# Moving half of a value projection, twelve top-key rounds, four zero fills and six weight splits between stages and engines of a hybrid decoder layer

## The chip, the cores and the metric

The kernel runs on one core of one Trainium2 chip. The time is the device time of one execution in microseconds (us), and a kernel's time is the median of its runs. The trace comes from one profiled execution. The engines are TensorE (PE, with its weight loads PEld), VectorE (DVE), ScalarE (ACT), GpSimd (POOL) and SyncE (SP, which issues most of the DMAs). Each engine works through its own instructions in the order in which the program lists them.

## The reference, cut to what matters

One decoder layer on 512 tokens of 1024 features, in float32. One input projection feeds two mixers side by side, an mLSTM (4 heads) and a sparse attention (8 heads, the 128 keys of highest indexer score per query). Their outputs go through one output projection, then a gated MLP with a width-3 convolution and a final norm.

```python
z = rms_norm(x) @ w_in                    # 1024 -> 3664 columns, split into:
# m_q, m_k (256 each), m_v, m_o (512 each), gates, a_q, a_k, a_v (512 each), indexer q, k, w
qk = silu(causal_dwconv(concat(m_q, m_k)))            # width 4
hm = mlstm_chunkwise(q, k, m_v, m_i + i_bias, m_f + f_bias)
hm = sigmoid(m_o) * rms_norm(hm)
score = sum_h relu(q_idx[h] @ k_idx.T / 8) * w_idx[h]  # causal
idx = top_k(score, 128)                                # then attention over these keys only
ha = softmax(a_q @ a_k[idx].T / 8 + rel_bias) @ a_v[idx]
x = x + concat(hm, ha) @ w_out
```

The top keys are not gathered: for each block of 128 queries the kernel strikes out the eight largest scores sixteen times and keeps as a mask which keys were struck.

## The kernel before, in words

Tokens go in four blocks of 128 (t = 0 to 3). A float32 product is made of three products of split operands: `split` rounds a tile to the high part on ScalarE (L122) and subtracts it for the low part (L123), on VectorE, or on GpSimd for weights whose index is in `on_pool`. Weight columns come in by DMA (`raw`, 1 MB each) and are split in pieces ahead of use: `take` hands out the split pieces of a step and puts the splits of later ones into a queue `later`, of which one entry is run after each step.

The order of the work is written out by `merge`: a list of main steps spread evenly over 0 to 1, and side lists with a range of their own; all are sorted by their place. `fm_steps` (four steps for 128 output columns, each 6 matmuls of 512 columns) and `tm_steps` (eight steps for 256 output columns, each 12 matmuls of 256 columns) make the main steps. The stages around the change are:

- the indexer's query stage (`to_iq`), with the first steps of `idx_steps` (the indexer's scores) beside it;
- the stage of the attention's projections (`to_aq`, `to_ak`, `to_av`), with the rest of the indexer's steps, the gates' first part, and the top keys of t = 1, 2 and the first part of t = 3 (`top_steps`: 16 times max, L510, and strike, L513, and then `keep`, L516). `att_[0]`, the ready step, makes the first queries and the first `ql` pair (`second`, L657);
- the attention's stage: four convolution projections (`to_conv`, 16 steps) and the mLSTM values (`to_mv`, 8 steps for each half), with the rest of the top keys of t = 3 and the attention's steps beside them. An attention step i puts the scores of item i (t, head) into one of three `lg` banks (L670 to L673), makes the numerators of item i - 1 (L695 on VectorE, L698 on ScalarE), transposes those of item i - 3 and multiplies those of item i - 4 with the values (L711). `second` makes the low part of the queries, two L657 for two heads. For t = 3, L704 on GpSimd needs the last `keep`. After the convolutions `silus` runs SiLU on `mq` and `mk`;
- the output gates' stage (`to_mo`, 16 steps), with the mLSTM's decays (`decays[2:]`), the split queries and keys (`parts`: L825 and L826 for keys, L834 to L836 for queries, L816 for the zeros that fill the other half of the low queries), the score steps (`qks`: two matmuls L844, L845, evicted at L847, L850), and the transposition of the attention's output (`to_mix`);
- the output projection and the mLSTM's heads, and then the MLP, which the change doesn't touch.

The stages are not separated by barriers: each engine goes on as far as its operands are there. The split indices are: 17 to 20 convolution, 21 to 24 values, 25 to 28 output gates, 29 to 36 output projection.

Of the kernel before, what the change touches and what calls it, by code (L numbers as in the profile page):

```python
# [11 lines left out]
F32R = mybir.dt.float32r  # L12
BF = mybir.dt.bfloat16
AF = mybir.ActivationFunctionType
OP = mybir.AluOpType

S, D, DFF, NB = 512, 1024, 2816, 4
# [27 lines left out]
def hybrid_layer(ctx: ExitStack, tc: tile.TileContext, a, out):  # L45
# [44 lines left out]
    def merged(main, *sides):  # L90
        merge(main, *sides, later=later)
        while later:
            later.popleft()()
# [84 lines left out]
    for c2 in range(NF // 2):  # L178
        add_raw(rows(a["w_down"], 2 * c2), [row_cut(0), row_cut(1)])
    sub_i, look = [0], [2]  # L180
    on_pool = set(range(6, 31)) | {35,37,39}

    def take(n=1):

# [317 lines left out]
    def top_steps(t):  # L502
        w = (t + 1) * 128
        acc = score[t][:, :w]

        m8 = {}

        def largest():
            m8[0] = small.tile([128, 8], F32, name="m8")
            nc.vector.max(m8[0], acc)  # L510

        def strike():
            nc.vector.match_replace(acc, m8[0], acc, TAKEN)  # L513

        def fin():
            nc.vector.tensor_scalar(keep[t][:, :w], acc, TAKEN, -BIG, op0=OP.not_equal, op1=OP.mult)  # L516
        return [largest, strike] * 16 + [fin]
# [86 lines left out]
    for c in range(4):  # L604
        main += fm_steps(H, to_iq(c), tok=((128, 512),))
    idx = idx_steps()
    merged(main, (0.0, 0.02, [params_consts]), (0.5, 0.55, [params_bias]), (0.0, 0.02, [misc_a]), (0.18, 0.2, [misc_b]),
          (0.3, 1.05, idx[:18]), (0.8, 0.85, [params_conv]))

    kS = big.tile([128, 8, S], F32R, name="kS", tag="B0")  # L610

# [21 lines left out]
    def zeros():  # L633
        nc.gpsimd.tensor_scalar(qlz.rearrange("p a b c -> p (a b) c"), ident[:, None, :].to_broadcast([128, 4, 128]), 0.0,
                                None, op0=OP.mult)

    def att_steps(ts):
# [14 lines left out]
        def second(p):  # L652

            t, c = divmod(p, 4)
            src = aqT[:, c, t * 128:(t + 1) * 128]
            for i, a_ in ((0, slice(0, 64)), (1, slice(64, 128))):
                nc.vector.tensor_tensor(qlz[a_, p % 2, i, :], src[a_], qp[p // 2][a_, c % 2, i, :].bitcast(F32), OP.subtract)  # L657

        def step(i):
            if i % 4 == 1 and i // 4 + 1 < n // 4:  # L660
                queries(i // 4 + 1)
            if i % 2 == 0 and i // 2 + 1 < n // 2:
                second(i // 2 + 1)
            if i < n:
                t, h = items[i]
# [56 lines left out]
        def costed(i):  # L722
            def f():
                step(i)
            f.cost = items[min(i, n - 1)][0] + 2.947
            return f
        def ready():
            zeros()
            queries(0)
            second(0)  # L730
        return [ready] + [costed(i) for i in range(n + 4)]

    main = []
# [2 lines left out]
    for c in range(4):  # L736
# [2 lines left out]
    att_ = att_steps(range(NB))  # L739
    top3 = top_steps(3)  # L740
    mm_tags[:] = ["mm", "mm", "av"][:3]
    merged(main, (0.0, 0.07, idx[18:]), (0.3, 0.5, gates_a), (0.07, 0.32, top_steps(1)), (0.32, 0.68, top_steps(2)),
           (0.68, 1.0, top3[:18]), (0.3, 0.32, [params_bias2]), (0.75, 0.76, [att_[0]]))


    mv = ap.tile([128, NB, 4, 130], F32, name="mv")
# [12 lines left out]
    def to_mv(c2):  # L759
        return lambda t, pz: nc.scalar.activation(mv[:, t, 2 * c2:2 * c2 + 2, :128],  # L760
                                                  pz.rearrange("p (h d) -> p h d", h=2), AF.Copy)
# [19 lines left out]
    def weight_steps():  # L781
# [28 lines left out]
        def zeros(h):  # L810

            b_ = own[h % 2][1]
            if h == 0:
                ql["two"] = ap.tile([128, 2, S], F32R, name="mql", tag="mk")
            ql[h] = ql["two"][:, h, :] if h < 2 else ap.tile([128, S], F32R, name="mql", tag=("ql", "score3")[h - 2])
            nc.gpsimd.tensor_scalar(ql[h][b_].rearrange("p (t c) -> p t c", t=NB),  # L816
                                    ident[b_, None, :].to_broadcast([64, NB, 128]), 0.0, None, op0=OP.mult)

        def keys(h):
            if h == 0:  # L820
                zeros(2)
                zeros(3)
            a_, b_ = own[h % 2]
            kh[h], src = part(h), mk[a_, h // 2, :]
            nc.scalar.activation(kh[h][a_], src, AF.Copy)  # L825
            nc.vector.tensor_tensor(kh[h][b_], src, kh[h][a_].bitcast(F32), OP.subtract)  # L826
            if h == 3:
                zeros(0)
                zeros(1)

        def queries(h):
            a_, b_ = own[h % 2]
# [24 lines left out]
    main = []  # L857
    for c in range(4):
        main += fm_steps(H, to_conv(c))
    for c2 in range(2):  # L860
        main += tm_steps(H, to_mv(c2))
    merged(main, (0.0, 0.32, top3[18:]), (0.403, 0.74, gates_b), (0.781, 0.957, decays[:2]), (0.7, 0.7, [silus]), (0.007, 1.0, att_[1:]))


    def head_steps(pair):
# [39 lines left out]
    def to_mix(src, mix, t):  # L905
        pt = bank("tp")
        for j in range(4):
            nc.tensor.transpose(pt[:, j * 128:(j + 1) * 128], src[:, j, :], ident)
        sl = slice(t * 128, (t + 1) * 128)
        split(mix[:, 0, :, sl], mix[:, 1, :, sl], pt.rearrange("p (j c) -> p j c", j=4))  # L910

    mm_tags[:] = ["mm", "mm", "av"]
    main = []
    for c2 in range(2):
        main += tm_steps(H, to_mo(c2))
    merged(main, (0.0, 0.057, decays[2:]), (0.1, 0.586, parts), (0.482, 1.0, qks),
           (0.238, 0.839, [lambda t=t: to_mix(ha[t], mixa, t) for t in range(NB)]))

    def gate_out(t):
        nc.scalar.activation(so[:, t, :], so[:, t, :], AF.Sigmoid)  # L920
# [201 lines left out]
```

## Time and profile before

| | |
|---|---|
| median of 3 runs (lowest to highest) | 688.69 us (688.48 to 689.21) |
| the profiled execution | 688.66 us, its span 686.9 us |
| mean granted TensorE clock | 0.986 of full speed |
| busy: TensorE, VectorE, ScalarE, GpSimd | 657.9, 404.6, 297.5, 169.1 us |

Times in the views are microseconds from the start of the span. A busy TensorE may still run at a lower clock, so its busy time is read together with the granted clock: 1.00 is 2.4 GHz and 0.50 is 1.2 GHz. VectorE's busy time includes the time in which a started instruction stands still.

### The profile page before, as it was taken

Reading aid. Unit: us, or ns where it says so; the run is one execution under the profiler, and the core shown is the slowest. Engines: PE = TensorE matmul, PEld = TensorE weight load, DVE = VectorE, ACT = ScalarE, POOL = GpSimd, SP = SyncE. Lnnn points to the kernel's source line nnn. Section 1 sums busy time; section 2 is a strip of 40 time slices with the busy share of each in tenths; the row PEclk is TensorE's granted clock in tenths of the full one; section 3 lists DMA queues with packets and bytes.
Section 4 is the critical chain, followed back from the end, with each engine's and each line's share of the span. In section 5 each row is a group of like instructions: output and inputs, shape, how many; then the busy total and the mean of one; then the engine's idle time right before and its main releaser. Section 6 shows DMA issues by size and latency. Waiting matters only on the chain.

```text
span 686.9 us, 8960 instructions
## 1 busy us (share of the span) xinstructions
PE 657.9 (96%) x3455; PEld 561.8 (82%) x3455; DVE 404.6 (59%) x735; ACT 297.5 (43%) x512; POOL 169.1 (25%) x166
## 2 busy tenths in 40 slices
PE   7999999699999779999999999999999999999996
PEld 5987889478999779889988888888888888888885
DVE  4689999896645766567456655555555653222234
ACT  5556265266573705345344444444444442111123
POOL 2132576132451814324010110101011020000023
PEclk9999999899999979999999999999999999999999
DMA  9321633011101111051132233311333133313102
GB/s 304 111 64 61 210 98 123 0 63 62 62 1 62 62 62 62 1 154 62 61 105 80 64 120 122 124 61 62 123 123 121 62 139 138 123 63 121 61 31 92
DMA packets 47194, 62.22 MB, mean 91 GB/s; under 512 B 3795, under 2 KB 40855, under 8 KB 47152
## 3 DMA queue, kind: packets, MB, share of 16 engines
q1 hardware_dynamic: 45488, 56.83, 24.9%
q0 software_dynamic: 944, 3.25, 1.5%
q10 hardware_dynamic: 720, 1.57, 0.6%
q8 instruction: 27, 0.44, 0.3%
q14 instruction: 15, 0.12, 0.1%
HBM read 59.53 MB, written 2.12 MB: 90 GB/s over the span
## 4 chain that ended last, share of the span: by engine, by line
PE 80%; DVE 14%; issue 2%; ACT 2%; POOL 1%; DMA 1%; POOLq 0%; DVEq 0%; ACTq 0%
PE bank_mm L192 9%; PE bank_mm L194 9%; PE bank_mm L193 9%; PE bank_av L194 4%; PE bank_av L192 4%; PE bank_av L193 4%; DVE score L513 4%; DVE m L510 3%; PE bank_av L711 2%; PE bank_lg L1051 2%; PE bank_lg L1052 2%; PE bank_lg L1050 2%; DVE score L495 2%; PE bank_mm L236 2%; PE bank_mm L237 2%; PE bank_mm L238 2%
## 5 line engine op out<-in xcount | busy, mean ns | idle before, releaser
L123 DVE TENSOR_TENSOR wlo<-raw,whi 128x1024 fp32r<-128x1024 f32 x72 | 89.4, 1246 | 118.5 <-ACT whi L122 118.5
L122 ACT ACTIVATE whi<-raw 128x1024 fp32r<-128x1024 f32 x100 | 104.6, 1051 | 85.4 <-PE bank_mm L1051 73.4
L192 PE MATMUL bank_mm<-fh,whi 128*128 128x512 f32 (+1 forms) x256 | 96.3, 376 | 0.0
L194 PE MATMUL bank_mm<-fh,wlo 128*128 128x512 f32 (+1 forms) x256 | 96.2, 376 | 0.0
L193 PE MATMUL bank_mm<-fl,whi 128*128 128x512 f32 (+1 forms) x256 | 96.2, 376 | 0.0
L123 POOL TENSOR_TENSOR wlo<-raw,whi 128x1024 fp32r<-128x1024 f32 x28 | 68.8, 2468 | 80.4 <-ACT whi L122 59.0
L1015 POOL TENSOR_TENSOR yc<-yc 128x512 f32<-128x512 f32 x22 | 28.4, 1292 | 213.4 <-DVE yc L999 213.4
L193 PEld LDWEIGHTS bank_mm<-fl,whi 128*128 128x128 f32 x256 | 48.2, 188 | 8.8
L194 PEld LDWEIGHTS bank_mm<-fh,wlo 128*128 128x128 f32 x256 | 48.2, 188 | 8.8
L192 PEld LDWEIGHTS bank_mm<-fh,whi 128*128 128x128 f32 x256 | 48.2, 188 | 8.6
L192 PE MATMUL bank_av<-fh,whi 128*128 128x512 f32 (+1 forms) x120 | 45.1, 376 | 0.0
L194 PE MATMUL bank_av<-fh,wlo 128*128 128x512 f32 (+1 forms) x120 | 45.0, 375 | 0.0
L193 PE MATMUL bank_av<-fl,whi 128*128 128x512 f32 (+1 forms) x120 | 45.0, 375 | 0.0
L192 PE MATMUL bank_mm<-hh,whi 128*128 128x512 f32 (+1 forms) x112 | 44.0, 393 | 0.0
L122 ACT ACTIVATE gh<-yc 128x512 fp32r<-128x512 f32 x22 | 13.9, 632 | 69.5 <-POOL yc L1015 69.5
L123 DVE TENSOR_TENSOR gl<-yc,gh 128x512 fp32r<-128x512 f32 x22 | 15.2, 693 | 47.4 <-ACT gh L122 47.4
L194 PE MATMUL bank_mm<-hh,wlo 128*128 128x512 f32 (+1 forms) x112 | 42.5, 380 | 0.0
L193 PE MATMUL bank_mm<-hl,whi 128*128 128x512 f32 (+1 forms) x112 | 42.4, 379 | 0.0
L236 PE MATMUL bank_mm<-whi,hh 128*128 128x256 f32 x128 | 38.8, 303 | 0.0
L237 PE MATMUL bank_mm<-whi,hl 128*128 128x256 f32 x128 | 37.2, 291 | 0.0
L238 PE MATMUL bank_mm<-wlo,hh 128*128 128x256 f32 x128 | 37.2, 291 | 0.0
L1008 ACT ACTIVATE yc<-yc 128x512 f32<-128x512 f32 x22 | 13.9, 632 | 42.6 <-DVE yc L999 42.6
(324 smaller groups left out, 1541.3 us busy)
## 6 DMA issues: line engine op xcount, KB each, us to landing
raw<-in_w_up_dram SPq DMA_DIRECT2D x22, 1024.0 KB, 5.1
raw<-in_w_in_dram SPq DMA_DIRECT2D x13, 1024.0 KB, 5.0
raw<-in_w_down_dram SPq DMA_DIRECT2D x11, 1024.0 KB, 5.0
raw<-in_w_out_dram SPq DMA_DIRECT2D x4, 1024.0 KB
T<-skew POOLq DMA_DIRECT2D x1, 2048.0 KB, 8.6
x<-in_x_dram SPq DMA_DIRECT2D x3, 512.0 KB, 5.4
out_dram<-xn SPq DMA_DIRECT2D x4, 256.0 KB, 2.1
out_dram<-xn ACTq DMA_DIRECT2D x4, 256.0 KB, 2.5
```

Of the source, the lines that this page charges most:

```text
L122: nc.scalar.activation(hv, src, AF.Copy)
L123: (eng or nc.vector).tensor_tensor(lv, src, hv.bitcast(F32), OP.subtract)
L192: nc.tensor.matmul(ps_, lh, rh, start=first, stop=False)
L193: nc.tensor.matmul(ps_, lh, rl, start=False, stop=False)
L194: nc.tensor.matmul(ps_, ll, rh, start=False, stop=last)
L236: nc.tensor.matmul(st["ps"], ah, wh[:, i, :], start=(k == 0), stop=False)
L237: nc.tensor.matmul(st["ps"], al, wh[:, i, :], start=False, stop=False)
L238: nc.tensor.matmul(st["ps"], ah, wl[:, i, :], start=False, stop=(k == 7))
L510: nc.vector.max(m8[0], acc)
L513: nc.vector.match_replace(acc, m8[0], acc, TAKEN)
L1008: nc.scalar.activation(ys[c][:, 0, :], ys[c][:, 0, :], AF.Silu)
L1015: nc.gpsimd.tensor_tensor(y[:, 0, :], y[:, 0, :], y[:, 1, :], OP.mult)
```

## The change

Half of the mLSTM values (`to_mv(1)`, eight main steps) are projected at the start of the output gates' stage and no longer in the attention's stage. Of the 33 top-key steps of t = 3, six and not eighteen come ahead of the attention's stage, and the other 27 are spread over its first half; before, the last 15 were spread over its first 0.32. The two index steps 16 and 17 go from the indexer's stage to the next. The second `ql` pair is made in the ready step and not in the attention's first step. The zeros of the low queries are made by ScalarE (a copy with scale 0) and not by GpSimd, and heads 0 and 1 now use the tiles that are free early, heads 2 and 3 the tile of the keys. The splits 25 to 30 go from GpSimd to VectorE.

```diff
@@ -178,7 +178,7 @@
     for c2 in range(NF // 2):
         add_raw(rows(a["w_down"], 2 * c2), [row_cut(0), row_cut(1)])
     sub_i, look = [0], [2]
-    on_pool = set(range(6, 31)) | {35,37,39}
+    on_pool = set(range(6, 25)) | {35,37,39}
 
     def take(n=1):
 
@@ -605,7 +605,7 @@
         main += fm_steps(H, to_iq(c), tok=((128, 512),))
     idx = idx_steps()
     merged(main, (0.0, 0.02, [params_consts]), (0.5, 0.55, [params_bias]), (0.0, 0.02, [misc_a]), (0.18, 0.2, [misc_b]),
-          (0.3, 1.05, idx[:18]), (0.8, 0.85, [params_conv]))
+          (0.3, 1.0, idx[:16]), (0.8, 0.85, [params_conv]))
 
     kS = big.tile([128, 8, S], F32R, name="kS", tag="B0")
 
@@ -659,7 +659,7 @@
         def step(i):
             if i % 4 == 1 and i // 4 + 1 < n // 4:
                 queries(i // 4 + 1)
-            if i % 2 == 0 and i // 2 + 1 < n // 2:
+            if i and i % 2 == 0 and i // 2 + 1 < n // 2:
                 second(i // 2 + 1)
             if i < n:
                 t, h = items[i]
@@ -728,6 +728,7 @@
             zeros()
             queries(0)
             second(0)
+            second(1)
         return [ready] + [costed(i) for i in range(n + 4)]
 
     main = []
@@ -739,8 +740,8 @@
     att_ = att_steps(range(NB))
     top3 = top_steps(3)
     mm_tags[:] = ["mm", "mm", "av"][:3]
-    merged(main, (0.0, 0.07, idx[18:]), (0.3, 0.5, gates_a), (0.07, 0.32, top_steps(1)), (0.32, 0.68, top_steps(2)),
-           (0.68, 1.0, top3[:18]), (0.3, 0.32, [params_bias2]), (0.75, 0.76, [att_[0]]))
+    merged(main, (0.0, 0.1, idx[16:]), (0.3, 0.5, gates_a), (0.1, 0.34, top_steps(1)), (0.34, 0.7, top_steps(2)),
+           (0.7, 0.97, top3[:6]), (0.3, 0.32, [params_bias2]), (0.75, 0.76, [att_[0]]))
 
 
     mv = ap.tile([128, NB, 4, 130], F32, name="mv")
@@ -810,23 +811,23 @@
         def zeros(h):
 
             b_ = own[h % 2][1]
-            if h == 0:
+            if h == 2:
                 ql["two"] = ap.tile([128, 2, S], F32R, name="mql", tag="mk")
-            ql[h] = ql["two"][:, h, :] if h < 2 else ap.tile([128, S], F32R, name="mql", tag=("ql", "score3")[h - 2])
-            nc.gpsimd.tensor_scalar(ql[h][b_].rearrange("p (t c) -> p t c", t=NB),
-                                    ident[b_, None, :].to_broadcast([64, NB, 128]), 0.0, None, op0=OP.mult)
+            ql[h] = ql["two"][:, h - 2, :] if h >= 2 else ap.tile([128, S], F32R, name="mql", tag=("ql", "score3")[h])
+            nc.scalar.activation(ql[h][b_].rearrange("p (t c) -> p t c", t=NB),
+                                 ident[b_, None, :].to_broadcast([64, NB, 128]), AF.Copy, scale=0.0)
 
         def keys(h):
             if h == 0:
-                zeros(2)
-                zeros(3)
+                zeros(0)
+                zeros(1)
             a_, b_ = own[h % 2]
             kh[h], src = part(h), mk[a_, h // 2, :]
             nc.scalar.activation(kh[h][a_], src, AF.Copy)
             nc.vector.tensor_tensor(kh[h][b_], src, kh[h][a_].bitcast(F32), OP.subtract)
             if h == 3:
-                zeros(0)
-                zeros(1)
+                zeros(2)
+                zeros(3)
 
         def queries(h):
             a_, b_ = own[h % 2]
@@ -857,9 +858,8 @@
     main = []
     for c in range(4):
         main += fm_steps(H, to_conv(c))
-    for c2 in range(2):
-        main += tm_steps(H, to_mv(c2))
-    merged(main, (0.0, 0.32, top3[18:]), (0.403, 0.74, gates_b), (0.781, 0.957, decays[:2]), (0.7, 0.7, [silus]), (0.007, 1.0, att_[1:]))
+    main += tm_steps(H, to_mv(0))
+    merged(main, (0.0, 0.5, top3[6:]), (0.403, 0.74, gates_b), (0.781, 0.957, decays[:2]), (0.7, 0.7, [silus]), (0.007, 1.0, att_[1:]))
 
 
     def head_steps(pair):
@@ -910,11 +910,11 @@
         split(mix[:, 0, :, sl], mix[:, 1, :, sl], pt.rearrange("p (j c) -> p j c", j=4))
 
     mm_tags[:] = ["mm", "mm", "av"]
-    main = []
+    main = tm_steps(H, to_mv(1))
     for c2 in range(2):
         main += tm_steps(H, to_mo(c2))
-    merged(main, (0.0, 0.057, decays[2:]), (0.1, 0.586, parts), (0.482, 1.0, qks),
-           (0.238, 0.839, [lambda t=t: to_mix(ha[t], mixa, t) for t in range(NB)]))
+    merged(main, (0.0, 0.05, decays[2:]), (0.08, 0.5, parts), (0.42, 1.0, qks),
+           (0.16, 0.6, [lambda t=t: to_mix(ha[t], mixa, t) for t in range(NB)]))
 
     def gate_out(t):
         nc.scalar.activation(so[:, t, :], so[:, t, :], AF.Sigmoid)
```

## Rows read from the trace of the kernel before

**Rows 1.** The page's busy times: us, share of the span, instructions.

```profile
PE 657.9 (96%) x3455; PEld 561.8 (82%) x3455; DVE 404.6 (59%) x735; ACT 297.5 (43%) x512; POOL 169.1 (25%) x166
```

**Rows 2.** Windows: stretch, length; busy of PE, PEld, DVE, ACT, POOL; clock; DMA.

```profile
116.80:128.00 11.20, 4.67 (x23) 3.38 (x22) 10.68 (x24) 3.33 (x5) 3.19 (x3) 0.87 0.10 35
128.00:132.00 4.00, 3.79 (x12) 3.12 (x12) 3.79 (x16) 1.67 (x7) 0.79 (x2) 0.51 0.00 0
132.00:137.00 5.00, 5.00 (x35) 4.32 (x34) 2.26 (x8) 3.09 (x10) 0.00 (x0) 1.00 0.00 0
137.00:155.30 18.30, 17.12 (x102) 14.01 (x101) 17.88 (x47) 10.97 (x34) 6.97 (x8) 1.00 0.18 59
233.00:248.00 15.00, 7.74 (x34) 6.98 (x35) 13.08 (x16) 4.76 (x7) 9.66 (x6) 0.66 0.36 135
218.90:262.00 43.10, 35.64 (x247) 33.06 (x246) 31.45 (x62) 18.02 (x25) 17.67 (x10) 0.88 0.14 50
```

**Rows 3.** Waits of TensorE: line, releaser, us in total, times, longest.

```profile
PE bank_lg L671 <- DVE ql L657: 6.1, 1, 6.1
PE bank_tp L844 <- DVE sc L850: 4.0, 1, 4.0
...
PE bank_tp L844 <- ACT part L835: 1.8, 1, 1.8
```

**Rows 4.** Timeline of GpSimd and VectorE, 104 to 156 us: start, length, instruction.

```profile
108.74 4.82 POOL L123 TENSOR_TENSOR wlo<-raw,whi 128x1024 fp32r<-128x1024 f32 x2
...
110.30 3.42 DVE L657 TENSOR_TENSOR ql<-qv,qd 64x128 fp32r<-64x128 f32 x2
...
126.41 0.59 DVE L657 TENSOR_TENSOR ql<-qv,qd 64x128 fp32r<-64x128 f32 x2
...
154.60 0.67 DVE L516 TENSOR_SCALAR keep<-score 128x512 bf16<-128x512 f32 x1
```

**Rows 5.** Timeline of ScalarE, VectorE and GpSimd in the output gates' stage.

```profile
226.95 2.57 ACT L825 ACTIVATE part<-mk 64x512 fp32r<-64x512 f32 x4
...
227.59 4.34 DVE L826 TENSOR_TENSOR part<-mk,part 64x512 fp32r<-64x512 f32 x2 [3.42 <-ACT part L825]
...
231.47 6.79 POOL L816 TENSOR_SCALAR mql<-ident 64x512 fp32r<-64x512 f32 x4
...
237.34 6.09 DVE L836 TENSOR_TENSOR mql<-mq,part 64x512 fp32r<-64x512 f32 x1
...
238.24 4.65 POOL L123 TENSOR_TENSOR wlo<-raw,whi 128x1024 fp32r<-128x1024 f32 x2
...
244.66 0.69 DVE L836 TENSOR_TENSOR mql<-mq,part 64x512 fp32r<-64x512 f32 x1
```

**Rows 6.** VectorE's groups by shape, 107 to 175 us: busy, mean ns, idle before.

```profile
L510 DVE MAX8 m<-score 128x8 f32<-128x512 f32 x16 | 11.1, 693 | 0.4
L513 DVE MATCH_REPLACE8 score<-m,score 128x512 f32<-128x512 f32 x16 | 10.8, 676 | 0.0
L695 DVE CUSTOM_DVE_ANT_0 l<-bank_lg,T 128x384 f32<-128x384 f32 x7 | 3.8, 555 | 0.1
```

**Rows 7.** Timeline of TensorE, six places of the attention's stage.

```profile
153.81 0.48 PE L192 MATMUL bank_mm<-hh,whi 128*128 128x512 f32 x1
...
155.28 0.34 PE L670 MATMUL bank_lg<-kS,qd 128*128 128x384 f32 x1
...
156.40 0.48 PE L192 MATMUL bank_mm<-hh,whi 128*128 128x512 f32 x1
...
175.57 0.34 PE L670 MATMUL bank_lg<-kS,qd 128*128 128x384 f32 x1
...
177.02 0.36 PE L236 MATMUL bank_mm<-whi,hh 128*128 128x256 f32 x1
...
178.53 0.39 PE L670 MATMUL bank_lg<-kS,qd 128*128 128x512 f32 x1
```

**Rows 8.** The page's group of weight splits on VectorE.

```profile
L123 DVE TENSOR_TENSOR wlo<-raw,whi 128x1024 fp32r<-128x1024 f32 x72 | 89.4, 1246 | 118.5 <-ACT whi L122 118.5
```

## The prediction, made before the result was known

> **What bounds the kernel now.** The busy table of the page comes first: TensorE is busy 96% of the span [rows 1]. So only three things can give time: the places where TensorE stands still, where it runs at the lower clock, and where another engine holds it up. The list of waits, TensorE's alone, names the places [rows 3]: 6.1 us on VectorE's `ql` (L657), and waits of the score step L844, 4.0 us on VectorE and 1.8 us on ScalarE. The windows place them [rows 2]. The first lies where the attention starts: from 116.8 to 128.0 us TensorE is busy 4.67 us of 11.20, then has 3.79 us of work at a mean clock of 0.51, that is at the lower level (1.2 GHz), which costs half of it, 1.9; a further 1.2 us are missing up to 155.3. Together 6.5 + 1.9 + 1.2 = 9.6 us. The others lie in the output gates' stage: from 233 to 248 us 7.3 us are missing, and a mean clock of 0.66 means that about 10.2 us of the window ran at the lower level; 4.0 of these were the last wait, so some 6.2 us of work cost 3.1 extra. Together 10.4 us. The prize is therefore about 20 us, in two places with different causes.
>
> **Why TensorE waits at the start of the attention.** VectorE is busy 10.68 of 11.20 us there and 17.88 of 18.30 in the window after [rows 2]. The second `ql` pair stands in VectorE's order behind rounds of max and strike, and starts only at 126.41 [rows 4], 6 us after TensorE came to it. VectorE stays the late engine until the last top-key instruction, the `keep` of L516, at 154.6 [rows 4].
>
> **Why it waits in the gates' stage.** VectorE's subtractions there are slow: two of L826 take 4.34 us, one of L836 takes 6.09, where the one at 244.66, of the same size, takes 0.69. Both long ones lie under GpSimd's work: two splits of 4.65 us begin at 238.24 and end at 242.89, and the 6.09 us end at 243.43 [rows 5]. The same is seen earlier: the `ql` pair at 110.30 takes 3.42 us in place of 0.59 and ends just behind GpSimd's split pair (108.74 to 113.56) [rows 4]. A subtraction from SBUF on VectorE stands still while GpSimd is inside an instruction. The Trainium skill's page "SBUF — State Buffer" (section "SBUF: two separate sides") has the rule: the shared port pair is an exclusive lock, and a VectorE instruction with two SBUF inputs waits for a GpSimd one that reads SBUF. By that rule a zero made by GpSimd costs VectorE up to its full length and one by ScalarE costs it nothing; the trace agrees with the first half, and the sum below uses the rows alone.
>
> **The change, gates' stage.** Four zeros of 6.79/4 = 1.7 us leave GpSimd [rows 5] and come to ScalarE; the nearest row is L825, 64x512 by ScalarE, 2.57/4 = 0.64 each, so 2.6 us. Six splits (indices 25 to 30) go from GpSimd (2.3 us each [rows 5]) to VectorE (1.24 each [rows 8]): 7.5 us, all in this stage. The second half of the values adds eight steps of TensorE. Such a step takes 178.53 - 177.02 = 1.51 us with the change of kind [rows 7], about 1.45 among its like: 11.6 us, which leave the attention's stage, so their sum is zero. What they bring is cover: the first score step stood after 8 of 16 main steps and now stands after 11 of 24, 4.4 us later, and the queries that it needs come at nearly the same place. The zeros for heads 0 and 1 now go where no keys have to be read first.
> VectorE's load over the stage: 31.45 us of 43.10 before [rows 2], less about 8.7 of standing still (4.34 - 1.37 = 3.0, 6.09 - 0.69 = 5.4, 0.3 elsewhere), plus 7.5: 30. ScalarE: 18.0 [rows 2], plus zeros 2.6, two more splits 2.1 (they fell in the stage before) and four evictions 1.5: 24. TensorE has 43.1 - 10.4 + 11.6 = 44. So nothing is near TensorE, and GpSimd does almost nothing there. I give back 1 us for a score step that finds a 1.24 us split ahead of its eviction on VectorE. Gain: 10.4 - 1 = 9.4 us; bounds 10.4 (all of it) and 5 (only the last wait goes, with half of the clock's cost, and the earlier waits come back as ScalarE's longer queue).
>
> **The change, attention's stage.** Twelve of the top-key instructions for the last rows, 0.69 (max) and 0.68 (strike) each [rows 6], go from ahead of the attention into its first half: 8.2 us. Nothing is saved on VectorE; what matters is what else is in its queue ahead of `keep`. I write out both orders by the fractions of `merged`. Before, `keep` stands between attention steps 14 and 15; after, between 20 and 21. The attention has three `lg` banks, so TensorE can't start step j before VectorE has done step j - 2. Before, `keep` ends at 155.3 and TensorE just then starts step 16 (the 384-wide L670 at 155.28 [rows 7]); after, at that moment it can start step 22. In between lie
> - TensorE: six attention steps from 1.12 us (155.28 to 156.40) to 1.45 (175.57 to 177.02) [rows 7], 7.9 in all; two more convolution steps of 1.47 (153.81 to 155.28) [rows 7], 2.9; a gate step 0.2. Sum 11.0 us.
> - VectorE: six evictions of at most 0.56 [rows 6] with their accumulator reads, 3.3 less the two narrower ones' 0.2, 3.1; three `ql` pairs of 0.59 [rows 4], 1.8; one output scaling 0.9 and the gate step 0.9 (estimates from their place in the same timeline). Sum 6.7 us.
> So `keep` would end at 155.3 + 6.7 = 162.0 with the same idle as before. VectorE stood idle 5.00 - 2.26 = 2.7 us from 132 to 137 [rows 2], because TensorE came back at 1.2 GHz; with strikes at hand and no such stop, I take half of that back: 160.6. The `ql` pairs of step 0 and 2 are now both in the first part, where GpSimd's split pair blocked one before by 2.8 us; it may block two or none, so that is zero with a bound of 2.8 either way. Gain: 11.0 - (160.6 - 155.3) = 5.7, less 0.7 for the tighter hand-over at the end, where the SiLUs now follow the last convolution by two steps: 5.0 us. Bounds: 9.6 (TensorE never waits) and 0 (`keep` comes 5.7 later through blocked pairs and waits of VectorE on TensorE).
> The remaining edits (two index steps later, the second `ql` pair in the ready step) I cost at nothing: VectorE's queue up to the first max holds the same instructions, and TensorE, which reaches the attention 2 us or more ahead of VectorE, covers them; without that cover it is two evictions, 1.1 us.
>
> **Sum.** The profiled execution took 688.66 us (span 686.9 and 1.8 around it), the median is 688.69: the same. 688.7 - 9.4 - 5.0 = 674.3 us.
>
> **Rivals.**
> *VectorE takes the whole gain of the attention's stage.* The wait is not removed, it is spread: top-key rounds stand denser among the evictions. For it: VectorE at 17.88 of 18.30 us [rows 2] with fewer rounds per step than it will have. Against: the sums 11.0 and 6.7. Time: 688.7 - 9.4 = 679.3.
> *All stops go in both stages.* For it: the work sums, if blocking by GpSimd in the first half ends too. Against: VectorE's total before `keep`. Time: 688.7 - 9.6 - 10.4 = 668.7.
> *ScalarE becomes late in the gates' stage.* Keys, queries and zeros all pass through it; 1.8 us were already a wait on it [rows 3]. Half of that stage's gain stays away: 688.7 - 5 - 5 = 678.7.
> *Slower: the clock falls in the first half of the attention.* If TensorE follows VectorE in short stops, it may be granted 1.2 GHz through them. From 116.8 to 160.6 it has about 38 us of work in 44; each us of work at the lower level costs 1 us more, so with 6 us of slack and 14.4 gained, the change loses from 20 us of work at 1.2 GHz on; with 26 us of it the time is 674.3 + 20 = 694.3. Against it: from 137 to 155.3 TensorE stood still 1.2 us in pieces and the clock stayed 1.00; it fell to 0.51 only behind the 6.1 us stop [rows 2, 3]. The Trainium skill, "TensorE: Matmul & The Clock Gate", section "A second HAM failure mode: psum-queue depth-cycling", tells of just this: frequent small stops between groups made the clock swing between its levels. No row here shows it for small stops.
>
> **Numbers.** The forecast 0.50; VectorE takes the gain 0.19; all stops go 0.11; ScalarE late 0.12; clock 0.08. The first four are all faster; 0.02 of them is kept for no change, when both lower bounds meet. A run of this kernel can tell about 0.2% (1.4 us). Faster 0.90, same 0.02, slower 0.08. Range 668.5 to 682.5: the forecast with its bounds and the three faster rivals, with 0.08 for the clock and the rest for tails outside.
>
> **What would show it.** Right: no GpSimd zero, and no split by it in the gates' stage; L826 and L836 at about 0.7 us each; no TensorE wait above 1 us at L844/L845; clock 1.00 through that stage. At the start of the attention, no 6 us wait on L657, but several of under 1.5 us on VectorE, and `keep` near 160 to 161. Wrong: `keep` later than 164, a clock of 0.5 anywhere between 117 and 260 us, or ScalarE as the releaser of L844.

## The result and the profile after

The changed kernel takes 680.59 us (median of 4 runs, 680.08 to 681.01), the kernel before in the same session 688.85 (688.48 to 689.21): a ratio of 0.988, 95% interval 0.9863 to 0.9897. It is 8.3 us faster; 14.4 were forecast. The profiled execution took 681.01 us, with a span of 679.3.

The page's busy row of the changed kernel, to be held against [rows 1]:

```profile
PE 656.2 (97%) x3455; PEld 560.0 (82%) x3455; DVE 398.9 (59%) x741; ACT 299.8 (44%) x516; POOL 147.5 (22%) x156
```

TensorE's waits in the changed kernel, 100 to 262 us (answers to [rows 3]):

```profile
PE bank_tp L845 <- DVE mixa L123: 4.8, 1, 4.8
PE bank_av L711 <- ACT pT L686: 2.7, 4, 0.7
PE bank_lg L670 <- DVE nm L695: 1.0, 2, 0.6
PE bank_tp L681 <- ACT l L698: 0.8, 1, 0.8
PE bank_av L711 <- DVE qv L718: 0.4, 1, 0.4
```

The 6.1 us stop at the start of the attention is gone; what is left there are stops of at most 0.8 us. In the gates' stage three waits became one, at the second score step, of 4.8 us. Lines behind the diff have moved by one: L826 is now L827, L836 is L837, L844 is L845.

Windows of the changed kernel (columns as in [rows 2]): the first half of the attention up to the `keep`, the rest of that stage, the gates' stage, and 2 us pieces around its stop.

```profile
116.80:159.50 42.70, 39.01 (x238) 32.07 (x237) 39.38 (x118) 26.16 (x76) 11.88 (x15) 1.00 0.11 36
159.50:203.96 44.46, 43.27 (x320) 38.57 (x319) 24.94 (x63) 28.67 (x56) 18.51 (x16) 1.00 0.15 48
203.96:254.07 50.11, 45.27 (x340) 43.95 (x339) 30.32 (x68) 22.88 (x34) 1.27 (x2) 0.93 0.18 64
...
222.00:224.00 2.00, 0.86 (x6) 0.42 (x4) 0.99 (x3) 1.96 (x3) 0.00 (x0) 1.00 0.00 0
224.00:226.00 2.00, 0.00 (x0) 0.00 (x0) 2.00 (x3) 1.95 (x4) 0.00 (x0) 1.00 0.00 0
226.00:228.00 2.00, 0.30 (x1) 0.30 (x2) 2.00 (x5) 1.72 (x3) 0.00 (x0) 0.64 0.30 31
228.00:230.00 2.00, 2.00 (x9) 2.00 (x9) 1.61 (x4) 0.00 (x0) 0.00 (x0) 0.50 0.87 354
230.00:232.00 2.00, 2.00 (x11) 2.00 (x11) 0.69 (x3) 0.00 (x0) 0.00 (x0) 0.50 0.34 139
```

The clock is 1.00 through the whole attention's stage. Behind the stop of the gates' stage it is at the lower level (0.50, 1.2 GHz) from 228 to 232 us. While TensorE stands still, from 222 to 226 us, ScalarE is busy in both pieces, 1.96 and 1.95 of 2.00 us; VectorE is in the second, 2.00, but only 0.99 in the first.

The timeline of the changed kernel, at places that answer to [rows 4, 5, 7], and then the stop itself:

```profile
107.94 3.46 DVE L657 TENSOR_TENSOR ql<-qv,qd 64x128 fp32r<-64x128 f32 x4
...
159.11 0.43 DVE L516 TENSOR_SCALAR keep<-score 128x512 bf16<-128x512 f32 x1
...
161.21 0.34 PE L670 MATMUL bank_lg<-kS,qd 128*128 128x384 f32 x1
...
214.19 0.69 DVE L827 TENSOR_TENSOR part<-mk,part 64x512 fp32r<-64x512 f32 x1 [0.59 <-ACT part L826]
...
220.09 0.68 DVE L837 TENSOR_TENSOR mql<-mq,part 64x512 fp32r<-64x512 f32 x1 [2.13 <-ACT part L835]
...
220.35 0.60 PE L908 MATMUL bank_tp<-ident,qv 128*128 128x128 f32 x4
...
222.23 0.39 PE L845 MATMUL bank_tp<-part 128*128 128x512 f32 x1
...
222.67 2.00 ACT L122 ACTIVATE whi<-raw 128x1024 fp32r<-128x1024 f32 x2
...
224.58 0.61 ACT L835 ACTIVATE part<-mq 64x512 fp32r<-64x512 f32 x1
...
225.21 0.63 ACT L836 ACTIVATE part<-mq 64x512 fp32r<-64x512 f32 x1
225.23 1.22 DVE L123 TENSOR_TENSOR wlo<-raw,whi 128x1024 fp32r<-128x1024 f32 x1
225.87 0.60 ACT L122 ACTIVATE mixa<-bank_tp 128x512 fp32r<-128x512 f32 x1
...
226.37 0.68 DVE L837 TENSOR_TENSOR mql<-mq,part 64x512 fp32r<-64x512 f32 x1
...
226.97 0.67 DVE L123 TENSOR_TENSOR mixa<-bank_tp,mixa 128x512 fp32r<-128x512 f32 x1
...
227.70 0.69 PE L845 MATMUL bank_tp<-part 128*128 128x384 f32 x1 [4.84 <-DVE mixa L123]
```

Read the last rows from the end. The second score step needs a `tp` bank. That bank holds the third transposed block of the attention's output (L908 at 220.35), and comes free when the block is split: high part on ScalarE at 225.87, low part on VectorE at 226.97. The wait names VectorE, but the low part needs the high part, and ScalarE had queries, two weight splits (2.00 us together) and the next head's queries ahead of the block in its order: it comes to the block about 5 us behind the transposition. VectorE adds some 0.5 us of its own, a subtraction (L837) that is done at 227.05, where the high part was ready at 226.47. The engine that is late is first of all ScalarE.

Where the time went by stage, for all kernels run. The attention's stage is taken from 116.80 us to the third decay matmul (L784 or L785), the gates' stage from there to the first matmul of the output projection. The moved value steps are taken out of either (1.44 us each, the distance of two L236 at 208.69 and 210.13; 11.5 for eight), so that the rows can be compared. The differences of the sums agree with those of the spans within 0.1 us. The times come from several sessions, in which the kernel before had medians of 688.78 to 689.53 us, so times that are within 0.7 us of each other are not told apart.

| kernel | time, us | attention's stage | gates' stage |
|---|---|---|---|
| before | 688.85 | 90.8 | 42.6 |
| changed | 680.59 | 87.2 | 38.6 |
| e1: changed, scores later | 676.83 | 86.9 | 35.5 |
| e2: changed, zeros on GpSimd | 677.81 | 87.0 | 35.9 |
| e3: changed, splits on GpSimd | 681.53 | 86.8 | 39.6 |
| e4: top-key edits alone | 680.09 | 82.0 | 43.0 |
| e5: all but the top-key edits | 688.00 | 94.7 | 38.6 |
| e6: GpSimd edits alone | 684.73 | 91.4 | 38.1 |
| e8: all but the moved values | 676.15 | 82.7 | 38.9 |
| e9: e1 and e2 together | 674.58 | 86.8 | 32.2 |
| e10: e9, half of the moved steps back | 677.11 | 90.0 | 31.8 |
| e11: e8, scores later | 679.96 | 82.9 | 42.5 |
| e12: e8, zeros on GpSimd | 674.30 | 82.5 | 36.3 |
| e13: e11 and e12 together | 677.46 | 82.6 | 39.7 |

So from the kernel before to the changed one the attention's stage gained 3.6 us (5.0 forecast) and the gates' stage 4.0 (9.4 forecast).

### The profile page after: what moved, and what is told of

Same layout as the page of the kernel before. It is cut to its first block, busy times and chain, and to the rows that moved or that the text cites. A ratio compares the mean times of both kernels' runs of the same rounds, so it can differ in the third digit from the quotient of the medians.

```text
span 679.3 us, 8957 instructions
## 1 busy us (share of the span) xinstructions
PE 656.2 (97%) x3455; PEld 560.0 (82%) x3455; DVE 398.9 (59%) x741; ACT 299.8 (44%) x516; POOL 147.5 (22%) x156
## 4 chain that ended last, share of the span: by engine, by line
PE 74%; DVE 16%; ACT 4%; issue 3%; POOL 1%; DMA 1%; POOLq 0%; DVEq 0%; ACTq 0%
PE bank_mm L192 9%; PE bank_mm L193 9%; PE bank_mm L194 9%; PE bank_av L192 4%; PE bank_av L193 4%; PE bank_av L194 4%; DVE score L513 3%; DVE m L510 3%; DVE score L495 2%; PE bank_lg L1052 2%; PE bank_lg L1050 2%; PE bank_lg L1051 2%; PE bank_mm L363 2%; PE bank_av L711 2%; PE bank_mm L945 1%
## 5 line engine op out<-in xcount | busy, mean ns | idle before, releaser
L123 DVE TENSOR_TENSOR wlo<-raw,whi 128x1024 fp32r<-128x1024 f32 x78 | 96.7, 1244 | 121.5 <-ACT whi L122 121.5
L194 PE MATMUL bank_mm<-fh,wlo 128*128 128x512 f32 (+1 forms) x248 | 93.1, 376 | 0.0
L193 PE MATMUL bank_mm<-fl,whi 128*128 128x512 f32 (+1 forms) x248 | 93.1, 375 | 0.0
L123 POOL TENSOR_TENSOR wlo<-raw,whi 128x1024 fp32r<-128x1024 f32 x22 | 54.2, 2465 | 75.9 <-ACT whi L122 58.6
L192 PE MATMUL bank_av<-fh,whi 128*128 128x512 f32 (+1 forms) x128 | 48.2, 376 | 0.0
L194 PE MATMUL bank_av<-fh,wlo 128*128 128x512 f32 (+1 forms) x128 | 48.1, 376 | 0.0
L193 PE MATMUL bank_av<-fl,whi 128*128 128x512 f32 (+1 forms) x128 | 48.1, 376 | 0.0
L236 PE MATMUL bank_mm<-whi,hh 128*128 128x256 f32 x112 | 33.0, 295 | 0.0
L237 PE MATMUL bank_mm<-whi,hl 128*128 128x256 f32 x112 | 32.0, 286 | 0.0
L238 PE MATMUL bank_mm<-wlo,hh 128*128 128x256 f32 x112 | 32.0, 286 | 0.0
```

Of the source, the lines that this page charges most:

```text
L123: (eng or nc.vector).tensor_tensor(lv, src, hv.bitcast(F32), OP.subtract)
L192: nc.tensor.matmul(ps_, lh, rh, start=first, stop=False)
L193: nc.tensor.matmul(ps_, lh, rl, start=False, stop=False)
L194: nc.tensor.matmul(ps_, ll, rh, start=False, stop=last)
L236: nc.tensor.matmul(st["ps"], ah, wh[:, i, :], start=(k == 0), stop=False)
L237: nc.tensor.matmul(st["ps"], al, wh[:, i, :], start=False, stop=False)
```

## The experiments

**e1, the scores later.** The changed kernel with one place moved.

```diff
-    merged(main, (0.0, 0.05, decays[2:]), (0.08, 0.5, parts), (0.42, 1.0, qks),
+    merged(main, (0.0, 0.05, decays[2:]), (0.08, 0.5, parts), (0.56, 1.0, qks),
```

> The changed kernel with the sixteen score steps spread over 0.56 to 1.0 of the gates' stage, not 0.42 to 1.0. Theory S: the 4.8 us stop comes from ScalarE's queue, in which the high part of the third transposed block (it holds the tp bank that the second score step needs) stands behind queries and two weight splits; ScalarE has work enough for the first half of the stage but not for its place in it. Then 3.4 more main steps (about 4.8 us) ahead of the first score take the stop to under 1 us, the clock stays 1.00, and the time falls by 4.8 and the clock's 3: 673 us. Rival V: VectorE or ScalarE is short over the whole stage, so the stop only moves to later scores: 679 to 681 us.

Measured: 676.83 us, ratio 0.9824 (0.9808 to 0.984). The 4.8 us wait became three of at most 1.2 us, and the clock still fell behind the first two (0.79 from 228 to 236 us). Moving the scores helps, as the queue theory says, but by 3.8 us where about 7.6 were expected: the block is late even for scores that come 3.4 main steps later.

**e2, the zeros on GpSimd again.**

```diff
-            nc.scalar.activation(ql[h][b_].rearrange("p (t c) -> p t c", t=NB),
-                                 ident[b_, None, :].to_broadcast([64, NB, 128]), AF.Copy, scale=0.0)
+            nc.gpsimd.tensor_scalar(ql[h][b_].rearrange("p (t c) -> p t c", t=NB),
+                                    ident[b_, None, :].to_broadcast([64, NB, 128]), 0.0, None, op0=OP.mult)
```

> The changed kernel with the four zeros on GpSimd again, in the new order. Theory S: 2.6 us leave ScalarE's queue ahead of the third block, the stop shrinks from 4.8 to about 2 us, 677 to 678 us. Rival P: GpSimd's 1.7 us zeros stand in VectorE's way (each of the L827 and L837 subtractions that meets one waits for its end) and the late queries make the stop as long or longer: 681 to 684 us.

Measured: 677.81 us, ratio 0.9837 (0.982 to 0.9854), as the queue theory had it, and the wait is 3.1 us in place of 4.8. Undoing this part of the change, and no other, gives back 2.8 us. ScalarE reaches the third block's high part at 223.87 in place of 225.87.

**e3, the splits 25 to 30 on GpSimd again.**

```diff
-    on_pool = set(range(6, 25)) | {35,37,39}
+    on_pool = set(range(6, 31)) | {35,37,39}
```

> The changed kernel with splits 25 to 30 on GpSimd again. Theory P (port): VectorE's subtractions stand still behind splits of 2.3 us as before the change, by 2 to 6 us in the stage, and the time is 682 to 686 us. Rival: with ScalarE as the late engine, VectorE's standing still is hidden and the time stays at 680 to 681 us.

Measured: 681.53 us, ratio 0.9892 (0.9877 to 0.9907), 0.9 us over the changed kernel, between the two: about 0.5 us above the rival's range and 0.5 us below the theory's. The subtractions do stand still again, as the timeline of this run shows, but ScalarE is the late engine behind them, and hides nearly all of it.

```profile
210.80 4.76 POOL L123 TENSOR_TENSOR wlo<-raw,whi 128x1024 fp32r<-128x1024 f32 x2 [0.33 <-ACT whi L122]
...
213.78 3.76 DVE L827 TENSOR_TENSOR part<-mk,part 64x512 fp32r<-64x512 f32 x3 [5.38 <-ACT part L826]
```

**e4, the top-key edits alone.** The kernel before with these edits; values, zeros and splits as before.

```diff
-          (0.3, 1.05, idx[:18]), (0.8, 0.85, [params_conv]))
+          (0.3, 1.0, idx[:16]), (0.8, 0.85, [params_conv]))
...
+            second(1)
...
-           (0.68, 1.0, top3[:18]), (0.3, 0.32, [params_bias2]), (0.75, 0.76, [att_[0]]))
+           (0.7, 0.97, top3[:6]), (0.3, 0.32, [params_bias2]), (0.75, 0.76, [att_[0]]))
...
-    merged(main, (0.0, 0.32, top3[18:]), (0.403, 0.74, gates_b), (0.781, 0.957, decays[:2]), (0.7, 0.7, [silus]), (0.007, 1.0, att_[1:]))
+    merged(main, (0.0, 0.5, top3[6:]), (0.403, 0.74, gates_b), (0.781, 0.957, decays[:2]), (0.7, 0.7, [silus]), (0.007, 1.0, att_[1:]))
```

> The kernel before with the top-key edits alone (six steps ahead of the attention, two index steps moved, second ql pair in the ready step); values, zeros and splits as before. The first part of the gain alone: the trace of the changed kernel gives 3.6 us up to the gates' stage, so 685 us, with the 4.0 us wait in the gates' stage unchanged. Rival: this part gives nothing without the moved values (27 steps over half of 32 main steps end later, at main step 16 and not 12, next to the last rows' attention): 688 to 690 us.

Measured: 680.09 us, ratio 0.987 (0.9854 to 0.9887): as fast as the whole change, and faster than either theory had it. The attention's stage gains 8.8 us, the gates' stage nothing; its waits (the list of this run) are those of before:

```profile
PE bank_tp L845 <- DVE sc L851: 3.5, 1, 3.5
...
PE bank_tp L845 <- ACT part L836: 1.8, 1, 1.8
PE bank_tp L846 <- POOL mql L817: 1.7, 1, 1.7
```

**e5, all but the top-key edits.** The changed kernel with these places and the index steps as before.

```diff
-    merged(main, (0.0, 0.5, top3[6:]), (0.403, 0.74, gates_b), (0.781, 0.957, decays[:2]), (0.7, 0.7, [silus]), (0.007, 1.0, att_[1:]))
+    merged(main, (0.0, 0.427, top3[18:]), (0.403, 0.74, gates_b), (0.781, 0.957, decays[:2]), (0.7, 0.7, [silus]), (0.007, 1.0, att_[1:]))
```

> The kernel before with the other edits alone: half of the values in the gates' stage and its new places, zeros by ScalarE, splits 25 to 30 on VectorE; the top-key rounds, index steps and ql pairs as before (the last 15 top-key steps over the same ten main steps). Theory 'cover' (the eight value steps, taken out of the attention's stage, cost about 5 us there, because they were work that TensorE had while VectorE was late): the start-of-attention stop stays, the stage from 116.8 us to the third decay product is about 5 us worse than before minus the 11.5 us of the moved steps, the gates' stage gains 4: 688 to 691. Rival 'sum is zero' (as the prediction had it): the attention's stage costs nothing and the gates' stage gains 4: 683 to 686.

Measured: 688.00 us, ratio 0.9985 (0.9975 to 0.9994), at the lower end of the cover theory's range and far from the rival's. The gates' stage gains its 4.0 us, and the attention's stage loses 3.9. Its first stop grew to 7.5 us.

**e6, the GpSimd edits alone.** The kernel before, with the zeros by ScalarE (in the new order of the tiles) and

```diff
-    on_pool = set(range(6, 31)) | {35,37,39}
+    on_pool = set(range(6, 25)) | {35,37,39}
```

> The kernel before with the GpSimd edits alone: zeros by ScalarE (with the new order of the tiles) and splits 25 to 30 on VectorE; values, places and top-key rounds as before. Theory 'port': the subtractions of 4.34 (two) and 6.09 us come to 0.7 each, and the score steps no longer wait 4 us on VectorE: 5 to 9 us faster, 680 to 684. Rival 'ScalarE's queue': zeros and two more splits stand in ScalarE's order ahead of the queries' high parts, so the score steps wait on ScalarE in their place, 3 us or more in one stop: 686 to 689.

Measured: 684.73 us, ratio 0.9941 (0.9925 to 0.9957): 4.1 us faster, between the two theories, since both work. All subtractions take 0.67 to 0.70 us, and the waits on VectorE's work come back as waits on ScalarE's (this run's list):

```profile
PE bank_tp L844 <- ACT part L835: 2.3, 1, 2.3
PE bank_tp L844 <- DVE mixa L123: 1.5, 1, 1.5
PE bank_tp L844 <- ACT mixa L122: 0.7, 1, 0.7
```

**e8, all but the moved values.** The changed kernel with the values in the attention's stage and the places of the gates' stage as before.

```diff
-    main += tm_steps(H, to_mv(0))
+    for c2 in range(2):
+        main += tm_steps(H, to_mv(c2))
...
-    main = tm_steps(H, to_mv(1))
+    main = []
...
-    merged(main, (0.0, 0.05, decays[2:]), (0.08, 0.5, parts), (0.42, 1.0, qks),
+    merged(main, (0.0, 0.057, decays[2:]), (0.1, 0.586, parts), (0.482, 1.0, qks),
...
```

The place of the transposed blocks (`to_mix`), in the line left out, is as before too.

> The changed kernel with the values kept in the attention's stage (and so the places of the gates' stage as before): top-key edits, zeros by ScalarE, splits 25 to 30 on VectorE. Theory 'cover plus port': 680.1 of the top-key edits alone, less the 5 to 9 us of the GpSimd edits: 671 to 675. Rival 'ScalarE's queue': with no moved steps as cover in the gates' stage the score steps wait on ScalarE, so the GpSimd edits bring under 3 us: 677 to 681.

Measured: 676.15 us, ratio 0.9815 (0.9798 to 0.9833), just over the upper end of the cover theory, since the GpSimd edits bring 3.9 us here and not 5 to 9. Their worth is the same as in e6, so the two parts add: 8.8 and 4.1 (e4, e6) make 12.9, and e8 is 12.6 faster than the kernel before. The moved values, with the places that go with them, are what the changed kernel loses against it: 4.4 us, and 3.3 from e6 to e5.

**e9, both cures of the one stop**: the edits of e1 and e2 together in the changed kernel.

> The changed kernel with both cures of its one stop: score steps from 0.56 in place of 0.42, and the four zeros back on GpSimd. Theory 'ScalarE's queue' (the 4.8 us stop is the third transposed block's high part standing behind queries and splits): the two cures are for one stop, later scores had left 1.7 us of waits there, so at most these go: 674.5 to 676.5, and no score step waits over 1 us. Rival 'they add' (3.8 and 2.8 us): 674 or less. Rival 'port': zeros on GpSimd hold up VectorE's subtractions, which the later scores no longer cover: 678 to 681.

Measured: 674.58 us, ratio 0.9792 (0.9777 to 0.9807), within the queue theory's range. No wait of a score step is over 0.5 us, and the window of the gates' stage shows TensorE busy 43.02 of 43.71 us at full clock:

```profile
203.59:247.30 43.71, 43.02 (x340) 41.52 (x340) 30.91 (x68) 20.49 (x30) 7.21 (x6) 1.00 0.21 73
```

Without the moved steps the stage is 32.2 us, 10.4 less than before: the whole loss that the prediction had found there.

**e10, half of the moved steps back** in the attention's stage, on top of e9.

```diff
-    main += tm_steps(H, to_mv(0))
+    mv1 = tm_steps(H, to_mv(1))
+    main += tm_steps(H, to_mv(0)) + mv1[:4]
...
-    main = tm_steps(H, to_mv(1))
+    main = mv1[4:]
```

> The changed kernel with scores from 0.56 and zeros on GpSimd (674.6 us), and four of the eight moved value steps put back at the end of the attention's stage. Theory 'cover' (the moved steps cost 5 us in the attention's stage, in proportion): the stage gets half of it back and the gates' stage, which has no stop of over 0.5 us left, keeps most of its own: 672 to 673. Rival 'cover is worth as much behind': 674 to 676.

Measured: 677.11 us, ratio 0.9825 (0.981 to 0.984), worse than both theories. The gates' stage keeps all it had (31.8), but the attention's stage is the longest of all with the top-key edits, 90.0. The timeline of this run shows one new stop: TensorE waits 1.66 us for the transposed numerators `pT`.

```profile
132.54 1.04 ACT L122 ACTIVATE whi<-raw 128x1024 fp32r<-128x1024 f32 x1
133.49 0.83 ACT L648 ACTIVATE qd<-qv 64x256 fp32r<-64x256 f32 x2
...
133.92 2.76 DVE L657 TENSOR_TENSOR ql<-qv,qd 64x128 fp32r<-64x128 f32 x2 [0.26 <-ACT qd L648]
...
134.35 0.28 ACT L686 ACTIVATE pT<-bank_tp 128x128 f32<-128x128 f32 x1
...
134.68 0.43 PE L711 MATMUL bank_av<-qv,pT 128*128 128x64 f32 x2 [1.66 <-ACT pT L686]
```

It is ScalarE's order again: a weight split and the next queries stand ahead of `pT`. A `ql` pair is also held up there, 2.76 us in place of 0.59 under a split of GpSimd (133.73 to 136.08), but it begins 0.9 us into TensorE's stop and ends 2 us behind it, so it is not what this stop waits for; it delays what VectorE does next. The windows show the clock behind the stop:

```profile
132.00:134.00 2.00, 1.02 (x7) 0.66 (x5) 1.74 (x8) 1.83 (x5) 0.27 (x1) 1.00 0.00 0
134.00:136.00 2.00, 1.32 (x10) 1.28 (x11) 2.00 (x1) 1.36 (x5) 2.00 (x1) 0.98 0.00 0
136.00:138.00 2.00, 2.00 (x6) 1.51 (x6) 1.94 (x7) 0.76 (x3) 1.66 (x5) 0.50 0.33 80
```

The price of a moved step is therefore not a constant. The rest of this stage's loss (the `keep` comes at 166.64 us) I have not traced.

**e11 and e13, the scores later where the values stay**: e8, and e12 below, with

```diff
-    merged(main, (0.0, 0.057, decays[2:]), (0.1, 0.586, parts), (0.482, 1.0, qks),
+    merged(main, (0.0, 0.057, decays[2:]), (0.1, 0.586, parts), (0.56, 1.0, qks),
```

> The kernel with all edits but the moved values (676.15 us), and scores from 0.56 in place of 0.482 of the sixteen main steps (1.2 steps or 1.8 us later). Theory 'ScalarE's queue': its waits of 2.3 and 1.5 us shrink by what the scores come later, and the clock falls for a shorter time: 673 to 675. Rival: the later scores crowd at the stage's end and wait there for their evictions: 676 to 678.

> The kernel with all edits but the moved values, zeros on GpSimd and scores from 0.56. Theory 'cover plus ScalarE's queue': no stop over 1 us is left in either stage, so it is the fastest of all: 669 to 673. Rival 'some cover is needed in the gates' stage': with no moved steps ahead of the queries a stop of 2 us or more stays there: 674 to 676.

Measured: 679.96 us, ratio 0.9868 (0.9852 to 0.9883), and 677.46, ratio 0.9829 (0.9814 to 0.9845): both over 3 us slower than with the scores at 0.482, and beyond what theory and rival gave. In e11's timeline the evictions of the first scores now stand in VectorE's order behind the low part of a weight split, which waits for ScalarE's 2.00 us, and the next block's transposition (L909) waits for the bank:

```profile
231.52 2.00 ACT L122 ACTIVATE whi<-raw 128x1024 fp32r<-128x1024 f32 x2
232.61 1.22 DVE L123 TENSOR_TENSOR wlo<-raw,whi 128x1024 fp32r<-128x1024 f32 x1 [1.04 <-ACT whi L122]
...
233.95 0.55 DVE L851 SCALAR_TENSOR_TENSOR sc<-bank_tp,sc 128x384 f32<-128x384 f32 x1
...
234.64 0.77 PE L909 MATMUL bank_tp<-ident,qv 128*128 128x128 f32 x4 [4.35 <-DVE sc L851]
```

**e12, the zeros on GpSimd where the values stay**: e8 with the edit of e2.

> The kernel with all edits but the moved values (676.15 us), and the four zeros on GpSimd again (splits 25 to 30 on VectorE). Theory 'ScalarE's queue': 2.6 us of zeros leave ScalarE ahead of the queries, the 2.3 us wait goes or shrinks: 673.5 to 675.5. Rival 'port': two or three subtractions stand under zeros of 1.5 us each and the score steps wait on VectorE: 676 to 679.

Measured: 674.30 us, ratio 0.9785 (0.9767 to 0.9802), within the queue theory's range, the lowest median of all, not to be told from e9. It is the changed kernel without two of its parts, the moved values (with their places) and the zeros on ScalarE: the top-key edits, the splits on VectorE and the new order of the zeros' tiles stay. It is 6.3 us faster than the changed kernel.

## Why the prediction was right, and where it was not

**The two losses** were where the prediction put them, and their sizes hold: e9 takes back 10.4 us in the gates' stage, e12 8.3 of the 9.6 in the attention's.

**The gates' stage, 9.4 us forecast, 4.0 measured.** That is below the prediction's own lower bound for this stage, 5; the total is inside the range because the attention's stage stayed well above its lower bound of 0. The step that failed is "ScalarE: 18.0, plus zeros 2.6, two more splits 2.1 and four evictions 1.5: 24 ... nothing is near TensorE". The sum is right (22.9 us in the window of the stage), and it is the wrong question: it is a mean over 50 us, while the second score step asks when ScalarE gets to one block. In the pieces from 222 to 226 us ScalarE is busy 3.91 of 4.00. The time lost is 4.84 us of waiting and the lower clock behind it. Two premises beside it failed too. The cover of 4.4 us did not come about, since the queries moved with the scores: ScalarE began head 0's queries 2.6 us before TensorE came to the first score step in the kernel before (230.17 and 232.81 us), and 2.8 us before it in the changed one (219.43 and 222.23). And the new places put the third transposed block ahead of the scores, which the prediction did not write out: before, it came behind the fourth score step (247.37 us):

```profile
247.80 0.67 PE L908 MATMUL bank_tp<-ident,qv 128*128 128x128 f32 x4
```

In the changed kernel it comes at 220.35 us, ahead of the first. What this block's place alone costs, no run tells. e2 takes work out of ScalarE's queue and brings 2.8 us, e1 asks for the block later and brings 3.8, and e9, which does both, 6.0. This was the third rival, "ScalarE becomes late in the gates' stage" (678.7): its mechanism is what happened, and its price of half the stage's gain (5 us kept, 4.0 measured) was nearly right. One of its grounds is doubtful: the 1.8 us that [rows 3] put down to ScalarE end with head 2's query (L835, 233.93 us), which the first score step does not read; its bank comes free with VectorE's low part of the first transposed block, which ends at 234.43 us, as near to the step's start at 234.57.

**The zeros.** "A subtraction from SBUF on VectorE stands still while GpSimd is inside an instruction" was too wide, and for zeros the trace did not agree. A row of the kernel before that the prediction left out shows it (timeline; [rows 5] has the zeros, 231.47 to 238.26 us, and the blocked pair of 4.34 us, under the split below):

```profile
226.18 5.21 POOL L123 TENSOR_TENSOR wlo<-raw,whi 128x1024 fp32r<-128x1024 f32 x2 [0.33 <-ACT whi L122]
...
232.30 1.40 DVE L826 TENSOR_TENSOR part<-mk,part 64x512 fp32r<-64x512 f32 x2
```

The pair under the splits takes 4.34 us, the pair under the zeros 1.40. Here it is GpSimd's splits that hold VectorE up by microseconds. The zeros cost something else, which the prediction did not name: a third wait of TensorE in this stage (the list of the kernel before), on the zeros themselves.

```profile
PE bank_tp L845 <- POOL mql L816: 1.7, 1, 1.7
```

It stands in e4's list too, and not in those of e2, e9, e12 and e13, which have the zeros on GpSimd, but in the new order of the tiles and with no split of GpSimd ahead of them; which of the two ends it, no run separates. The move to ScalarE was not needed for it, and cost 2.8 us (e2).

**The moved values.** "11.6 us, which leave the attention's stage, so their sum is zero. What they bring is cover" failed too. With the other edits the same, moving them costs the attention's stage 4.4 us (e8 82.7, changed 87.2) and brings the gates' stage, with its new places, 0.3 (38.9, 38.6). Of the 4.4, 2.8 are plain idle time of TensorE (4.88 us of that stage in the changed kernel, 2.04 in e8); the rest I have not placed. Part of the loss was inside the prediction's sum without a name: it counted two more convolution steps ahead of the `keep`, where with the values there would have been six. The cover is worth something only where the queue is cured and the scores come later: 32.2 us in e9 against 39.7 in e13 and 36.3 in e12; in the whole kernel's time e9 is no faster than e12.

**The attention's stage, 5.0 forecast, 3.6 measured.** The mechanism was right. The `keep` ends at 159.54 us (160.6 forecast); step 22 starts at 161.21, where 155.28 + 11.0 would have been its time before, a gain of 5.1 (5.7 forecast). The term that was too small is the hand-over behind it: 1.4 us lost in place of 0.7. From 159.5 us on TensorE lacks 1.2 of 44.46 us, where in the kernel before it lacked nothing from 155.3 us on. The blocked `ql` pairs, put at zero with a bound of 2.8, came out near it: the two pairs of the ready step took 3.46 us together, where the first alone had taken 3.42.

**The other rivals.** VectorE does not take the whole gain of the attention's stage. Not all stops go. The clock did not fall in the first half of the attention: 3.7 of 42.70 us are missing there in stops of at most 0.8 us, and the granted clock is 1.00. The Trainium skill's rule ("TensorE: Matmul & The Clock Gate", section "A second HAM failure mode: psum-queue depth-cycling") of frequent small stops is not borne out by these rows. In e10 the clock fell behind a stop of 1.66 us, in e1 behind stops of 0.56 and 1.16 us.

**The signs.** L827 and L837 at 0.7 us each, no GpSimd zero or split in the stage, no 6 us wait on L657: right. No wait of over 1 us at L845, and full clock in the gates' stage: wrong, and the clock of 0.50 there is one of the signs that the prediction had named against itself. Of the stops left in the attention's stage most are on ScalarE's work (3.5 us in five) and not on VectorE's (1.4 in three). The splits' term (VectorE takes them at 1.24 us each) brings 0.9 us (e3). All parts together: 8.8 from the top-key edits and 4.1 from the GpSimd edits, less 3.3 for the moved values (e6 to e5, which owe nothing to the changed kernel's own time), make 9.6, and 8.3 were measured.

## What to carry to other kernels

An engine's busy share of a stage does not say whether it is late: write out what stands in its order ahead of the one instruction that the bound engine asks for, here ScalarE's splits and queries ahead of one transposed block. Work of the bound engine beside a slower one has a price where it stands; moving it to another stage is not free until the rows show that the new stage waits for it and the old one does not. Time each part of a compound change alone: here one part was worth all of it, and two of the others, with their places, cost 6.3 us together (e12), of which nothing shows in the total.

## What the hardware showed that was not expected

GpSimd's two-input splits hold up VectorE's two-input subtractions (4.34 us for a pair, [rows 5]); its one-input zero fill does so far less. In e2's timeline a subtraction of 0.75 us (0.69 elsewhere) lies wholly inside the first of two fills of 1.49 us each:

```profile
217.69 3.06 POOL L817 TENSOR_SCALAR mql<-ident 64x512 fp32r<-64x512 f32 x2 [3.88 <-DVE part L827]
218.09 0.75 DVE L837 TENSOR_TENSOR mql<-mq,part 64x512 fp32r<-64x512 f32 x1 [0.49 <-ACT part L835]
```

In the same run two of VectorE's weight splits took 3.07 us beside the two other fills, in place of 1.24 us each. Whether the second input is what makes the difference, no run separates: the fill is another operation, shorter and on half the partitions.

The Trainium skill, "SBUF — State Buffer", section "SBUF: two separate sides", has the shared port pair locked for the whole of a GpSimd instruction that reads SBUF against a VectorE instruction with two SBUF inputs, and the fill reads `ident` from there. By that the subtraction would have begun its work only at 219.18 us, when the first fill ends; it was done at 218.84. The measurement decides.

The granted clock: after stops of up to 0.8 us it stayed at 1.00 from 116.8 to 159.5 us in the changed kernel; in e10, where TensorE was busy 2.34 us of the four up to 136, it was 0.50 (1.2 GHz) in the two that follow; in e1, where TensorE was busy 2.28 us of the four up to 230, it was 0.50 in the two that follow.
